# Two tile pairs without blocks at the start of two swiglu layers, and their block sums cut into steps

## The chip, the cores and the metric

One of the cores of one Trainium2 chip runs the kernel. The metric is the device time of one execution in microseconds (us), as the median of several runs. TensorE (PE) multiplies matrices, VectorE (DVE) and ScalarE (ACT) do the elementwise work, SyncE (SP) issues the loads of weights. "PEld" in the profile is TensorE loading the stationary operand.

## The reference

A block of a diffusion transformer with two layers works on 256 latent and 256 context tokens of width 1024, in float32. Each layer has a swiglu, a mixer (a short convolution in layer 0, grouped-query attention in layer 1) and another swiglu. Before each stands a modulated RMS norm, after each a gated residual sum.

```python
def _modulate(t, g, shift, scale):
    return _rms(t, g) * (1 + scale) + shift

def _swiglu(h, w13, w2):
    gte, up = jnp.split(h @ w13, 2, axis=-1)
    return (jax.nn.silu(gte) * up) @ w2
...
lat = lat + 0.5 * mod[:, 0, 2] * _swiglu(_modulate(lat, norm_g[i, 0], ...), ffn_w13[i, 0], ffn_w2[i, 0])
```

The hidden width is 2816, that is 22 tiles of 128 for the gate and 22 for the up part. The four swiglu layers are, in order of time, (layer 0, first), (layer 0, second), (layer 1, first), (layer 1, second). The first three work on all 512 tokens, the last on the 256 latent ones.

## The kernel before

The activations stand transposed: 128 features on the partitions, tokens along the free axis; the 512 tokens are two halves s = 0 (latent) and s = 1 (context). Every float32 product is made of three fast ones: each operand is split into a high part (ScalarE copies it to the rounded type) and a low part (VectorE subtracts the high part), `split` at L91 to L93, and `mm3` (L112 to L118) issues high*high, high*low and low*high. A product in the text below is one of these three matmuls.

A swiglu runs over the hidden tiles in thirds of 8, 7 and 7. "Tile pair" i is gate tile i and up tile i. `ffn` (L600) makes a pair in one of two ways.

- Without blocks: `load_w` loads and splits the weights (1024 x 256), `w13_mm` (L511) runs over the eight 128-deep slices of the 1024 features, for gate (`pg`) and up (`pu`): 2 x 8 x 3 = 48 products for each token half of 256 columns, 96 in all. `w13_post` (L517) takes silu, multiplies and splits the result.
- With blocks: `Pair` (L525) uses Winograd's form of Strassen's algorithm on 2 x 2 blocks: weights A11, A12, A21, A22 (feature half by gate or up), operand blocks B[feature half, token half]. It needs seven block products of 4 x 3 = 12 matmuls, 84 in all, and sums of blocks: S1 to S4 of the weights (VectorE, L548 to L557, into the tile `ws`, of which there is one), T1 to T4 of the operand (`Blocks.sums`, L314 to L330). Its steps are `head` (A11*B00 and A12*B10, first token half alone), `five` (S1*T1), `six` (S2*T2, S4*B11), `seven` (S3*T3) and `four` (A22*T4). `p` and `q` are its accumulators.

The operand blocks come from the norm before: `tail_norm` (L386) queues work that `flush` runs later. For s = 0 the blocks are made while the projection before still runs its last products; for s = 1 `both_parts` (L409) makes the inverse norm (TensorE sums squares, L231, ScalarE takes the root, VectorE the reciprocal, TensorE spreads it, L242), then two blocks (`block`, L290: VectorE scales to `t`, ScalarE adds the shift and writes `hr`, `bh` and VectorE `bl`), then all block sums.

The second and third swiglu (`ffn(0, 1, ...)` and `ffn(1, 0, ...)`) start at L607 with one pair without blocks: its first token half, then `flush` (the whole norm of s = 1 and the sums), then the next two pairs are loaded, split and summed and their heads run, then the second token half of the first pair. The first swiglu doesn't take this branch, nor does the last.

Buffers: three for raw weights (`wr`), four for halves of split weights (`wh`, `wl`), two for A22 (`w4h`, `w4l`), 16 for operand blocks and their sums, six PSUM banks for accumulators (one each for pg, pu, p, q). Loads are issued by SyncE in the program's order, each when its buffer is free. The text of the kernel gives the order of priority; a scheduler then sets each engine's fixed order, in which the engine works, and the semaphores. So the order of the lines is not that of the instructions. The modulation vectors are reduced on VectorE (L136) in spare places (`tick`).

Of the kernel before, what the change touches and what calls it, by code (L numbers as in the profile page):

```python
# [9 lines left out]
F32 = mybir.dt.float32  # L10
# [6 lines left out]
P = 128  # L17
D = 1024
KT = D // P
S = 256  # L20
# [19 lines left out]
def hybrid_kernel(ctx: ExitStack, tc: tile.TileContext, a: dict, out: bass.AP):  # L40
# [13 lines left out]
    def nm(s):  # L54
        uid[0] += 1
        return f"{s}{uid[0]}"
# [29 lines left out]
    def load_raw(src, n=2048):  # L86
        raw = wp.tile([P, 2048], F32, name=nm("wr"), tag="wr", bufs=3)
        nc.sync.dma_start(raw[:, :n], src)
        return raw
# [194 lines left out]
    class Blocks:  # L284
# [26 lines left out]
        def blk(self, key, k):  # L311
            return tuple(t[:, k * S : k * S + S] for t in self.t[key])

        def sums(self):  # L314
            r = self.raw
            b11, b12, b21, b22 = r[0, 0], r[0, 1], r[1, 0], r[1, 1]
            tt = nc.vector.tensor_tensor

            def keep(key, src):
                hi, lo = self.t[key] = hot("th"), hot("tl")  # L320
                split(hi, lo, src)

            tt(out=b11, in0=b12, in1=b11, op=ALU.subtract)
            keep("T1", b11)
            tt(out=b12, in0=b22, in1=b12, op=ALU.add)
            tt(out=b22, in0=b22, in1=b11, op=ALU.add)
            keep("T2", b22)
            tt(out=b21, in0=b21, in1=b22, op=ALU.subtract)
            keep("T3", b12)
            keep("T4", b21)  # L330

    class FirstBlocks(Blocks):

# [52 lines left out]
    def tail_norm(l, j, h):  # L386

        box = {}

        def tail(m, c0, c1):  # L390
            square_add(m, c0, c1)
            if m == KT - 1:
                if not box:
                    box["A"] = scale_of(l, j)
                    box["B"] = mod_ready(l, 3 * j)
                s = c0 // S

                def inv():
                    return rms_inv(s, (accs[s], accs[s, "last"]))

                def rest(part, ri):

                    if isinstance(h, Blocks):
                        h.block(s, part, box["A"], box["B"], ri, fine=s == 0 and part == 0)
                    else:
                        for k in range(4 * part, 4 * part + 4):
                            norm_k(s, k, h, box["A"], box["B"], ri)

                def both_parts():  # L409
# [115 lines left out]
    class Pair:  # L525
# [4 lines left out]


        def __init__(self, src, h):
            self.h = h
            raw = load_raw(src)
            a21, a22, a11, a12 = (raw[:, i * T2 : i * T2 + T2] for i in range(4))
            tt = nc.vector.tensor_tensor
            sm = wp.tile([P, 2048], F32, name=nm("ws"), tag="ws", bufs=1)
            s1, s2, s3, s4 = (sm[:, i * T2 : i * T2 + T2] for i in range(4))
            self.w = {}

            def keep(keys, src):
                hi, lo = half()
                split(hi, lo, src)
                for i, key in enumerate(keys):
                    self.w[key] = [t[:, i * T2 : i * T2 + T2] for t in (hi, lo)]

            keep(("A11", "A12"), raw[:, 1024:])
            tt(  # L548
                out=sm.rearrange("p (a b c) -> p a b c", a=2, b=2)[:, :, 0, :],
                in0=a21.unsqueeze(1).to_broadcast([P, 2, T2]),  # L550
                in1=raw[:, T2 : 3 * T2].rearrange("p (a c) -> p a c", a=2),
                op=ALU.subtract,
            )
            tt(out=s2, in0=a11, in1=s1, op=ALU.subtract)
            keep(("S1", "S2"), sm[:, :1024])
            tt(out=s4, in0=a12, in1=s2, op=ALU.subtract)
            keep(("S3", "S4"), sm[:, 1024:])  # L557
# [42 lines left out]
    def ffn(l, b, h, tot, gate, tail, gs=(), ev=1.5):  # L600
        gs = list(gs)
        i0 = 0
        for t, n in enumerate(THIRDS):
            between = ()
            if tot == T2:
                heads = []
                if t == 0 and not gs:  # L607

                    w = load_w(a["w13"][l, b, 0])
                    gs = [new_pair("g")]  # L610
                    pp = psum("pg"), psum("pu")
                    w13_mm(pp, w, h, range(KT), 0, S)
                    flush()
                    for i in (1, 2):
                        heads.append(Pair(a["w13"][l, b, i], h))
                        heads[-1].head()
                    w13_mm(pp, w, h, range(KT), S, T2)
                    w13_post(pp, gs[0], 0, T2)
                prev = None
                for i in range(len(gs), n):  # L620
                    if t == 0 and not heads and i in AS_IS[l, b]:
                        w = load_w(a["w13"][l, b, i])
                        pp = psum("pg"), psum("pu")
# [543 lines left out]
```

## Time and profile before

| | us |
|---|---|
| median of 3 runs | 1614.27 (1613.15 to 1616.92) |
| profiled execution | 1611.37 |
| its span, first to last instruction | 1609.5 |
| second swiglu: first product to fourth pair's first product | 569.82 to 607.11 |
| third swiglu: the same | 924.40 to 963.06 |

A page of the profile gives each engine's busy time and share, the chain of work that ended last (followed back from the last instruction) and the costliest groups of instructions. The views by time have one row for a run of equal instructions: start, time from the first's start to the last's end, engine, line, operation, output<-inputs, sizes, count, and in brackets the idle time before it and what ended that. The view by windows has, for each stretch, its length, then busy time and count of each engine, the clock that TensorE was granted (1.00 is full speed), the share of the DMA engines in use and GB/s. Matmul records overlap in time: one of 128x256 is shown with 0.28 us, while the next starts 0.12 us later.

### The profile page before, as it was taken

The numbers are of one execution on the slowest core, as the hardware profiler recorded it, in microseconds if no ns is written. First come the engines' busy times: TensorE is split into PE (matmuls) and PEld (weight loads), VectorE is DVE, ScalarE is ACT, GpSimd is POOL, SyncE is SP. The second block draws the span as 40 slices with busy tenths as digits, with TensorE's granted clock in tenths as the row PEclk, the third lists the DMA queues.
The fourth block names the chain that finished last, engine by engine and source line by source line (L and its number), as shares of the span: only waits on it lengthen the run. The fifth ranks groups of instructions, "written<-read, shape, count | busy, mean of one in ns | idle before, by whom it ended". The sixth has DMA issues, their size and how long they took to land.

```text
span 1609.5 us, 25613 instructions
## 1 busy us (share of the span) xinstructions
PE 1576.1 (98%) x10566; PEld 1450.1 (90%) x10566; DVE 1332.4 (83%) x2035; ACT 722.2 (45%) x1110; POOL 0.2 (0%) x4
## 2 busy tenths in 40 slices
PE   9999999999999999999999999999999999899999
PEld 6788998999888889899899889889899897789999
DVE  4988778879998889799797999898898789965554
ACT  5532452544322365335255465245254455454443
POOL 0000000000000000000000000000000000000000
PEclk9999999999999999999999999999999999999999
DMA  8456235234565513353433413452432463755453
GB/s 320 162 183 209 80 122 180 90 135 152 177 221 186 180 41 117 132 183 100 168 120 115 154 54 131 172 195 96 156 129 96 180 214 108 270 201 185 169 194 109
DMA packets 38277, 248.77 MB, mean 155 GB/s; under 512 B 5136, under 2 KB 6928, under 8 KB 12304
## 3 DMA queue, kind: packets, MB, share of 16 engines
q1 hardware_dynamic: 35712, 245.38, 43.7%
q10 hardware_dynamic: 2448, 1.76, 0.4%
q8 instruction: 82, 1.34, 0.3%
q14 instruction: 35, 0.29, 0.1%
HBM read 244.77 MB, written 1.05 MB: 153 GB/s over the span
## 4 chain that ended last, share of the span: by engine, by line
PE 82%; DVE 12%; DMA 3%; ACT 2%; issue 1%; DVEq 0%; ACTq 0%; SPq 0%
PE py L117 7%; PE py L116 7%; PE py L118 7%; PE p L116 6%; PE p L118 6%; PE p L117 6%; PE q L118 5%; PE q L116 5%; PE q L117 5%; DVE junk L136 4%; DVE wl L93 3%; PE pg L117 2%; PE pg L118 2%; PE pg L116 2%; PE pu L117 2%; PE pu L118 2%
## 5 line engine op out<-in xcount | busy, mean ns | idle before, releaser
L92 ACT ACTIVATE wh<-wr 128x1024 fp32r<-128x1024 f32 (+2 forms) x274 | 274.4, 1014 | 395.0 <-PE py L117 108.7
L93 DVE TENSOR_TENSOR wl<-wr,wh 128x1024 fp32r<-128x1024 f32 (+2 forms) x274 | 318.2, 1167 | 97.0 <-ACT wh L92 96.4
L136 DVE CUSTOM_DVE_ANT_0 junk<-wr,scbc,modb 128x1024 bf16<-128x1024 f32 x236 | 302.5, 1282 | 39.6 <-DMA wr<-in_modT 37.0
L117 PE MATMUL py<-gl,wh 128*128 128x512 f32 (+1 forms) x746 | 263.2, 353 | 0.0
L116 PE MATMUL py<-gh,wh 128*128 128x512 f32 (+1 forms) x746 | 263.1, 353 | 0.0
L118 PE MATMUL py<-gh,wl 128*128 128x512 f32 (+1 forms) x746 | 262.9, 352 | 0.0
L93 DVE TENSOR_TENSOR wl<-ws,wh 128x1024 fp32r<-128x1024 f32 x112 | 136.8, 1223 | 27.3 <-ACT wh L92 27.0
L118 PEld LDWEIGHTS py<-gh,wl 128*128 128x128 f32 x746 | 141.1, 189 | 19.1
L116 PEld LDWEIGHTS py<-gh,wh 128*128 128x128 f32 x746 | 141.2, 189 | 18.6
L117 PEld LDWEIGHTS py<-gl,wh 128*128 128x128 f32 x746 | 141.2, 189 | 18.0
L92 ACT ACTIVATE wh<-ws 128x1024 fp32r<-128x1024 f32 x112 | 117.8, 1057 | 76.4 <-PE p L117 34.2
L116 PE MATMUL p<-th,wh 128*128 128x256 f32 x448 | 126.8, 283 | 0.0
L117 PE MATMUL p<-tl,wh 128*128 128x256 f32 x448 | 126.8, 283 | 0.0
L118 PE MATMUL p<-th,wl 128*128 128x256 f32 x448 | 126.6, 283 | 0.0
L117 PE MATMUL q<-bl,wh 128*128 128x256 f32 x336 | 95.2, 283 | 0.0
L116 PE MATMUL q<-bh,wh 128*128 128x256 f32 x336 | 95.1, 283 | 0.0
L118 PE MATMUL q<-bh,wl 128*128 128x256 f32 x336 | 95.1, 283 | 0.0
L438 DVE SCALAR_TENSOR_TENSOR x<-py,G,x 128x256 f32<-128x256 f32 x168 | 74.2, 480 | 21.4 <-PE py L118 21.2
L116 PEld LDWEIGHTS p<-th,wh 128*128 128x128 f32 x448 | 86.0, 192 | 0.5 <-ACT sg L584 0.2
L117 PEld LDWEIGHTS p<-tl,wh 128*128 128x128 f32 x448 | 86.0, 192 | 0.3
L118 PEld LDWEIGHTS p<-th,wl 128*128 128x128 f32 x448 | 85.9, 192 | 0.0
L116 PE MATMUL pg<-hh,wh 128*128 128x256 f32 (+1 forms) x240 | 75.8, 316 | 4.6 <-ACT hh L260 4.6
(236 smaller groups left out, 4001.3 us busy)
## 6 DMA issues: line engine op xcount, KB each, us to landing
wr<-in_w SPq DMA_DIRECT2D x88, 1024.0 KB, 4.9
wr<-in_modT SPq DMA_DIRECT2D x67, 1024.0 KB, 4.9
wr<-in_w2b SPq DMA_DIRECT2D x32, 896.0 KB, 4.6
wr<-in_w2a SPq DMA_DIRECT2D x16, 1024.0 KB, 4.9
wr<-in_cw_cx SPq DMA_DIRECT2D x8, 1024.0 KB, 4.9
wr<-in_mod SPq DMA_DIRECT2D x5, 1024.0 KB, 7.4
wr<-in_cw_b SPq DMA_DIRECT2D x4, 1024.0 KB, 4.8
wr<-in_cw_out SPq DMA_DIRECT2D x4, 1024.0 KB, 4.9
```

The lines of the kernel that those rows point to most:

```text
L92: nc.scalar.activation(out=hi, in_=src, func=AF.Copy)
L93: nc.vector.tensor_tensor(out=lo, in0=src, in1=hi.bitcast(F32), op=ALU.subtract)
L116: nc.tensor.matmul(ps, wh, mh, start=first, stop=False, **kw)
L117: nc.tensor.matmul(ps, wh, ml, start=False, stop=False, **kw)
L118: nc.tensor.matmul(ps, wl, mh, start=False, stop=last, **kw)
L136: nc.vector.tensor_tensor_reduce(out=junk, in0=raw[:, j * D : j * D + D], in1=scbc[:, v, :], scale=1.0, scalar=modb[:, l, col : col + 1], ...
L438: nc.vector.scalar_tensor_tensor(out=x[:, m, s * S : s * S + S], in0=ps[:, o : o + S], scalar=g[:, m, s : s + 1], in1=x[:, m, s * S : s * ...
```

## The change

The second and third swiglu begin with two pairs without blocks (0 and 1) and one head (pair 2), instead of one and two. The order of priority is now: first half of pair 0, norm of s = 1, load of pair 1 and its first half, T1; second half of pair 0; load of pair 2, T2, S1 and S2; second half of pair 1; head of pair 2, T3 and T4, S3 and S4 and A22. Both kinds of sums are cut into steps that the caller names (`sums(n)`), and the norm no longer makes the operand's sums itself.

```diff
-        def sums(self):
+        def sums(self, n):
...
+            if n == 0:
+                tt(out=b11, in0=b12, in1=b11, op=ALU.subtract)
+                keep("T1", b11)
+            elif n == 1:
+                tt(out=b12, in0=b22, in1=b12, op=ALU.add)
+                tt(out=b22, in0=b22, in1=b11, op=ALU.add)
+                keep("T2", b22)
+            else:
+                tt(out=b21, in0=b21, in1=b22, op=ALU.subtract)
+                keep("T3", b12)
+                keep("T4", b21)
...
                     for part in range(2):
                         rest(part, ri)
-                    if isinstance(h, Blocks):
-                        h.sums()
...
         def __init__(self, src, h):
-            self.h = h
-            raw = load_raw(src)
...
+            self.h, self.w = h, {}
+            self.raw = load_raw(src)
+            self.keep(("A11", "A12"), self.raw[:, 1024:])
...
+        def sums(self, n):
...
+            if n == 0:
+                self.sm = sm = wp.tile([P, 2048], F32, name=nm("ws"), tag="ws", bufs=1)
...
+                self.keep(("S1", "S2"), sm[:, :1024])
+                return
+            sm = self.sm
+            tt(out=sm[:, 3 * T2 :], in0=a12, in1=sm[:, T2:1024], op=ALU.subtract)
+            self.keep(("S3", "S4"), sm[:, 1024:])
...
-                    w = load_w(a["w13"][l, b, 0])
-                    gs = [new_pair("g")]
-                    pp = psum("pg"), psum("pu")
-                    w13_mm(pp, w, h, range(KT), 0, S)
+                    w = [load_w(a["w13"][l, b, 0])]
+                    gs = [new_pair("g") for _ in range(2)]
+                    pp = [(psum("pg"), psum("pu")) for _ in range(2)]
+                    w13_mm(pp[0], w[0], h, range(KT), 0, S)
                     flush()
-                    for i in (1, 2):
-                        heads.append(Pair(a["w13"][l, b, i], h))
-                        heads[-1].head()
-                    w13_mm(pp, w, h, range(KT), S, T2)
-                    w13_post(pp, gs[0], 0, T2)
+                    w.append(load_w(a["w13"][l, b, 1]))
+                    w13_mm(pp[1], w[1], h, range(KT), 0, S)
+                    h.sums(0)
+                    w13_mm(pp[0], w[0], h, range(KT), S, T2)
+                    w13_post(pp[0], gs[0], 0, T2)
+                    heads.append(Pair(a["w13"][l, b, 2], h))
+                    h.sums(1)
+                    heads[0].sums(0)
+                    w13_mm(pp[1], w[1], h, range(KT), S, T2)
+                    w13_post(pp[1], gs[1], 0, T2)
+                    heads[0].head()
+                    h.sums(2)
+                    heads[0].sums(1)
...
                         pr = Pair(a["w13"][l, b, i0 + i], h)
+                        pr.sums(0)
+                        pr.sums(1)
                         pr.head()
```

More of the change, by code (lines that the diff above doesn't have):

```diff
@@ L321, in keep @@
                 split(hi, lo, src)
[L323 to L330, printed above, removed]
+            if n == 0:
[9 more added lines that the diff above has]
+                keep("T4", b21)
     class FirstBlocks(Blocks):
@@ L532, in __init__ @@
         def __init__(self, src, h):
-            self.h = h
-            raw = load_raw(src)
-            a21, a22, a11, a12 = (raw[:, i * T2 : i * T2 + T2] for i in range(4))
-            tt = nc.vector.tensor_tensor
[L537 to L557, printed above, removed]
+            self.h, self.w = h, {}
@@ new lines, in __init__, with keep @@
+            self.raw = load_raw(src)
+            self.keep(("A11", "A12"), self.raw[:, 1024:])
+        def keep(self, keys, part):
+            hi, lo = half()
+            split(hi, lo, part)
+            for i, key in enumerate(keys):
+                self.w[key] = [t[:, i * T2 : i * T2 + T2] for t in (hi, lo)]
+        def sums(self, n):
+            a21, a22, a11, a12 = (self.raw[:, i * T2 : i * T2 + T2] for i in range(4))
+            tt = nc.vector.tensor_tensor
+            if n == 0:
+                self.sm = sm = wp.tile([P, 2048], F32, name=nm("ws"), tag="ws", bufs=1)
+                tt(
+                    out=sm.rearrange("p (a b c) -> p a b c", a=2, b=2)[:, :, 0, :],
+                    in0=a21.unsqueeze(1).to_broadcast([P, 2, T2]),
+                    in1=self.raw[:, T2 : 3 * T2].rearrange("p (a c) -> p a c", a=2),
+                    op=ALU.subtract,
+                )
+                tt(out=sm[:, T2:1024], in0=a11, in1=sm[:, :T2], op=ALU.subtract)
+                self.keep(("S1", "S2"), sm[:, :1024])
[3 more added lines that the diff above has]
+            self.keep(("S3", "S4"), sm[:, 1024:])
```

## Prediction

> **What bounds the kernel now.** I read the page first: span, busy line, chain of work that ended last.
>
> ```profile
> span 1609.5 us, 25613 instructions
> PE 1576.1 (98%) x10566; PEld 1450.1 (90%) x10566; DVE 1332.4 (83%) x2035; ACT 722.2 (45%) x1110; POOL 0.2 (0%) x4
> PE 82%; DVE 12%; DMA 3%; ACT 2%; issue 1%; DVEq 0%; ACTq 0%; SPq 0%
> ```
>
> TensorE is nearly always busy and holds 82% of the chain, so a change gains only where TensorE stands or runs slowly. The view by windows shows the two stretches that the change rewrites, from the first product of a swiglu to the first product of its fourth tile pair. They differ from an ordinary stretch (608 to 618).
>
> ```profile
> core 0: us, PE busy (x) PEld busy (x) DVE busy (x) ACT busy (x) POOL busy (x), PEclk, DMA share, GB/s
> 569.80:607.10 37.30, 33.76 (x254) 32.61 (x253) 32.24 (x43) 25.18 (x41) 0.00 (x0) 0.91 0.17 57
> 583.20:589.00 5.80, 5.25 (x23) 4.96 (x24) 5.80 (x7) 3.72 (x7) 0.00 (x0) 0.50 0.00 0
> 608.00:618.00 10.00, 10.00 (x84) 9.95 (x84) 9.96 (x14) 6.11 (x10) 0.00 (x0) 1.00 0.31 107
> 924.40:963.10 38.70, 35.08 (x255) 33.54 (x254) 35.42 (x48) 25.89 (x44) 0.00 (x0) 0.91 0.17 55
> 930.50:933.70 3.20, 3.20 (x15) 3.20 (x16) 3.20 (x5) 0.68 (x1) 0.00 (x0) 0.50 0.98 325
> 944.00:947.40 3.40, 3.27 (x15) 3.27 (x16) 3.40 (x5) 0.00 (x0) 0.00 (x0) 0.50 0.02 5
> ```
>
> An ordinary product (128x256) costs 10.00/84 = 0.119, say 0.12 us. Up to the fourth pair the program has 240 products in each stretch: 96 of the pair without blocks, 84 of the second, 60 of the third. That is 28.8 us; the stretches take 37.3 and 38.7. Part of the rest are waits, part the clock: in three windows the granted clock is 0.50 and a product takes twice as long. The timeline of TensorE names the waits of the second swiglu, the view of its waits from 924 to 964 those of the third (total, times, longest).
>
> ```profile
> 579.95 0.28 PE L118 MATMUL q<-bh,wl 128*128 128x256 f32 x1
> 583.25 0.58 PE L116 MATMUL pg<-bh,wh 128*128 128x256 f32 x1 [3.03 <-ACT bh L92]
> 584.55 0.58 PE L117 MATMUL pg<-bl,wh 128*128 128x256 f32 x1 [0.49 <-DVE bl L93]
> ```
>
> ```profile
> PE ss L231 <- ACT sq L214: 1.2, 1, 1.2
> PE pg L117 <- DVE bl L93: 1.0, 2, 0.5
> PE pg L116 <- ACT bh L92: 0.6, 1, 0.6
> PE q L116 <- ACT th L92: 0.4, 1, 0.4
> PE ss L242 <- DVE ri L240: 0.3, 1, 0.3
> ```
>
> In the second swiglu TensorE runs out of products that need only the first token half and stands 3.03 us until the second half's block is split. In the third it stands 3.5 us in smaller pieces.
>
> **Products.** A tile pair without blocks is 96 products, one with blocks 84. One pair per swiglu changes kind: 12 more products, 1.44 us, twice: **+2.9 us**, certain. In exchange TensorE has more to do before it needs the second token half: 96 products of two pairs, where it had 48 of one pair and 24 of the next pair's head. 24 more are 2.9 us, about the length of the 3.03 us wait.
>
> **Second swiglu.** In the compiled order TensorE takes after its 24 products with the first block: four column sums, two products with the second block, two of the new pair, then the rest. TensorE takes products in order, so the two of the new pair hold all behind them. Now six products of the second pair's head (p) fill that place. The rows, of TensorE, ScalarE and VectorE:
>
> ```profile
> 572.58 0.28 PE L118 MATMUL pu<-bh,wl 128*128 128x256 f32 x1
> 572.70 0.28 PE L231 MATMUL ss<-ones,acc 128*128 128x1 f32 x2
> ...
> 578.30 0.60 PE L242 MATMUL ss<-ident,ri 128*128 128x128 f32 x4
> ```
>
> ```profile
> 572.88 0.40 ACT L214 ACTIVATE sq<-x 128x256 f32<-128x256 f32 x1
> 573.19 1.04 ACT L92 ACTIVATE bh<-hr 128x1024 fp32r<-128x1024 f32 x1
> 574.21 0.26 ACT L236 ACTIVATE rs<-ss,eps_t 128x2 f32<-128x2 f32 x1
> 574.37 1.05 ACT L92 ACTIVATE wh<-ws 128x1024 fp32r<-128x1024 f32 x1
> ```
>
> ```profile
> 574.27 1.23 DVE L93 TENSOR_TENSOR bl<-hr,bh 128x1024 fp32r<-128x1024 f32 x1 [0.67 <-ACT bh L92]
> 575.41 0.16 DVE L240 RECIPROCAL ri<-rs 128x2 f32<-128x2 f32 x1
> 575.49 1.20 DVE L93 TENSOR_TENSOR wl<-ws,wh 128x1024 fp32r<-128x1024 f32 x1
> ```
>
> The split of the new pair's second weight half takes the place of the one at 574.37. A weight split of the fourth pair (A22) now stands ahead of the first block on ScalarE and VectorE; its load is issued when the first pair's weights are split, as now, so it shifts that chain by no more than about 0.3 us. Hence the weights are ready at 574.37 + 1.05 + 0.3 = 575.7. From 572.7 TensorE has four column sums (0.28 each by the row, 1.1) and two products (0.24) to do in 3.0 us: **1.65 us of new idle time**. After that nothing is late: the weights' low part is ready near 577.0 (575.49 + 1.20 + 0.3) and needed near 579.2 (22 products and the transposes, 0.6, after 575.9); TensorE then has 46 products, to 584.7, while the second half's block, ready at 583.20 and 584.5 now (rows above), comes 0.3 to 0.9 earlier, because two splits of sums of weights (1.2 us each on VectorE) no longer stand between its steps. The waits of 3.03 and 0.49 go. With them goes the slow clock of 583 to 589: 23 products, 2.8 us at 0.12, kept TensorE 5.25 us, so 2.5 us. Sum: 1.44 + 1.65 - 3.5 - 2.5 = **-2.9 us**, if no new slow window comes.
>
> ```profile
> 926.90:930.30 3.40, 2.04 (x16) 1.64 (x14) 2.65 (x6) 2.88 (x8) 0.00 (x0) 1.00 0.01 2
> 940.55:943.96 3.41, 2.05 (x13) 1.44 (x11) 3.41 (x4) 2.52 (x3) 0.00 (x0) 1.00 0.00 0
> ```
>
> These are the 3.4 us just before the slow windows at 930.5 and 944: 2.04 and 2.05 us busy was enough for the clock to fall. In the changed kernel the 3.4 us around the new idle time are about as busy, so I give a slow window there an even chance. One costs 3.4 us at 15 products (1.8 us): 1.6 us. The bounds are -2.9 and -1.3; I take the middle, **-2.1**. [...]
>
> **Third swiglu.** The waits of 3.5 us go, since the first-half products of two pairs are enough until the second half's blocks are split, and with them both slow windows: 30 products, 3.6 us, took 6.5: 2.9 us. 1.44 us come on top. New waits: ScalarE's second weight split stands right behind the first quarter of the first block and waits for its buffer, held by the projection's last product at about 924.5. Everything behind it on ScalarE (three quarters of that block, the next block) stands with it, and VectorE, which needs their results, too.
>
> ```profile
> 922.04 0.68 DVE L556 TENSOR_TENSOR ws<-wr,ws 128x512 f32<-128x512 f32 x1
> 922.64 1.26 DVE L250 SCALAR_TENSOR_TENSOR t<-x,A,ss 128x256 f32<-128x256 f32 x3
> ```
>
> ```profile
> 923.31 0.90 ACT L299 ACTIVATE bh<-t,mod 128x256 fp32r<-128x256 f32 x2
> ```
>
> The split (1.05) ends near 925.6, and ScalarE's steps of 0.4 us run on from there instead of 923.7. TensorE follows in order: 0.1 for that split, 0.35 for the second quarter's high part (926.4), 0.25 for its low part, 0.45 for the new pair's first low weights (VectorE, behind that quarter's low part: 928.1), 0.45 for the second (behind the norm's reciprocal: near 932.3); small ones make it 1.8 us. VectorE's subtraction for the third pair (the 0.68 row's place is taken by one of 1.22) delays the first t by 0.3, within that. Sum: 1.44 + 1.8 - 3.5 - 2.9 = **-3.2**. Followed from start to end instead (924.4, 252 products of 0.12, 1.7 for sums and transposes, 1.8 waits) the stretch ends at 958.1 against 963.1: -5.0. The two differ by small gaps of the present run that I can't name and that may remain. Bounds -3.2 and -5.0; I take **-4.1**.
>
> **At nothing:** VectorE and ScalarE lose the new pair's share (some 5 us on VectorE per swiglu: subtractions of weights, one and a half splits, three steps of its end); off the chain here, hidden beside 33 us of products. Two modulation reductions (1.28 each, below) move from the third swiglu's pairs to just before its norm; the norm's sums on TensorE end after them.
>
> ```profile
> L136 DVE CUSTOM_DVE_ANT_0 junk<-wr,scbc,modb 128x1024 bf16<-128x1024 f32 x236 | 302.5, 1282 | 39.6 <-DMA wr<-in_modT 37.0
> ```
>
> The block sums in their steps: the compiled order puts the first of them where it was, after the blocks; the first use comes later by 24 products or more, so they have over 3 us of slack. Outside the two stretches all orders are as before.
>
> **Sum:** -2.1 - 4.1 = -6.2 us. On the profiled execution, 1611.37 (1.9 around its span of 1609.5), that is 1605.2. The median shown is 1614.27, 2.9 higher, so I forecast **1608.1**.
>
> **Rivals.**
> - *The clock stays up, small gaps go too:* -2.9 - 5.0 = -7.9, **1606.4**. For it: each new wait but the first is shorter than those now. Against: the rows at 926.9 and 940.55. [...]
> - *Other waits take the place of the old:* the third swiglu's third load. SyncE's list of loads is the same in number and order; this one goes into the first pair's buffer and is issued at 916.54. VectorE's subtraction of it now stands ahead of the first block.
>
> ```profile
> 909.29 0.33 SPq L88 DMA_DIRECT2D wr<-in_w  x1
> ...
> 916.54 0.33 SPq L88 DMA_DIRECT2D wr<-in_w  x1
> ```
>
> ```profile
> 916.50 0.63 ACT L92 ACTIVATE w4h<-wr 128x512 fp32r<-128x512 f32 x1 [0.91 <-DMA wr<-in_w]
> ```
>
> ```profile
> wr<-in_w SPq DMA_DIRECT2D x88, 1024.0 KB, 4.9
> ```
>
>   At 4.9 it lands at 921.4, before its turn; at the 7.2 of the load of 909.29 at 923.7, 2 us late, with one slow window 3.6 us: -2.6 in all, **1611.7**. Behind it stand the block's steps, for which TensorE waits.
> - *No gain:* the sums stay where they were and the 2.9 us of products eat what is filled: **1614**.
> - *Slower: stalls moved, not filled.* The new pair's weights go through the same two queues as the blocks. If they are ready after the second half's block (583.2; I reckon 577.0, in the third near 932 against 940), the waits of 3.5 + 3.5 stay, 2.9 is paid, and each stretch has one slow window more: 2.9 + 3.2 = +6.1, **1620.4**. For it: VectorE is busy 35.42 of 38.7 us. Against: these splits stand ahead of that block's on both engines.
>
> **How the numbers follow.** A measurement tells 0.2% (3.2 us) from no change. Forecast (-4 to -8) 0.50; clock stays up 0.17; other waits 0.18, of which 0.07 beyond 3.2 us; no gain 0.06; slower 0.09. Faster 0.50 + 0.17 + 0.07 = 0.74, same 0.11 + 0.06 = 0.17, slower 0.09. The range leaves a tenth on each side: 1603.5 (the clock's rival and 2.9 more, the scatter between the profiled execution and the median) to 1614 (no gain).
>
> **What would show it.** The wait for bh at the second swiglu (3.03) is gone; instead some 1.7 us before a pg product, for wh on ScalarE. The stretches to the fourth pair last 35.2 and 34.6 us. At most one window at 0.50 in the first, none in the second. 24 more products. It is wrong if TensorE still waits over 1 us for the second half's blocks, if the third swiglu's first block starts over 1 us later, or if a half-clock window follows in both.

## The result, and the profile after

The changed kernel takes 1606.18 us, the median of four executions (1604.79 to 1607.14); the kernel before, in four on the same chip, 1613.71 (1612.65 to 1616.92). The ratio is 0.9946, with a 95% interval of 0.9928 to 0.9963. By the medians that is 7.5 us less, by the ratio 8.7 (6.0 to 11.6); the forecast was 6.2 less. The time is 1.9 below the forecast and inside its range, 0.6 of that because the kernel before came out at 1613.71 and not at 1614.27. On another chip, beside the last experiments, it was 1605.73 against 1614.83, a ratio of 0.9937 (0.9922 to 0.9952). The ratios are not quite the quotients of the medians; gains below that are given with a range are worked out from the ratios.

The page of the profiled execution (1606.83 us) of the changed kernel: span, busy line, chain of work that ended last.

```profile
span 1605.0 us, 25629 instructions
PE 1578.0 (98%) x10590; PEld 1451.0 (90%) x10590; DVE 1322.5 (82%) x2021; ACT 717.7 (45%) x1100; POOL 0.2 (0%) x4
PE 88%; DVE 8%; ACT 1%; DMA 1%; issue 1%; ACTq 0%; SPq 0%; DVEq 0%
```

TensorE has the 24 products more (10590 for 10566), VectorE 14 instructions and 9.9 us less. TensorE's share of the chain goes from 82 to 88%. That is some 90 us, far more than was gained: the chain runs through other instructions than before, and its shares don't measure the gain.

The view by windows of the two rewritten stretches, first product to the fourth pair's first product:

```profile
core 0: us, PE busy (x) PEld busy (x) DVE busy (x) ACT busy (x) POOL busy (x), PEclk, DMA share, GB/s
572.28:607.21 34.93, 33.61 (x266) 33.23 (x265) 28.41 (x38) 23.30 (x38) 0.00 (x0) 0.95 0.18 61
923.54:957.36 33.82, 33.07 (x266) 31.94 (x265) 32.51 (x47) 25.60 (x42) 0.00 (x0) 1.00 0.20 68
```

37.29 became 34.93 us, 38.66 became 33.82: -2.4 and -4.8, together -7.2. Each holds 11 or 12 product records more than before and is still shorter; the granted clock rose from 0.91 to 0.95 and 1.00. TensorE's waits, first in the second swiglu's stretch, then in the third's:

```profile
PE pg L116 <- ACT wh L92: 0.7, 1, 0.7
PE ss L231 <- ACT sq L214: 0.5, 1, 0.5
```

```profile
PE pg L118 <- DVE wl L93: 0.4, 1, 0.4
PE pu L118 <- DVE wl L93: 0.2, 1, 0.2
```

The waits for the second half's norm and blocks (3.03 + 0.49, and 3.5 in pieces) are gone; 1.2 and 0.6 us of others stand in their place.

The two profiled executions differ by only 4.5 us, less than the stretches' 7.2. Of the 2.7 us between, 2.5 are clock near the start, which the change leaves alone; the parts between and behind the two stretches differ by -1.0 and +1.2. The same 6.8 us near the start, in the kernel before and in the changed one:

```profile
14.83:21.66 6.83, 6.75 (x33) 2.92 (x34) 1.98 (x5) 1.50 (x4) 0.00 (x0) 1.00 0.85 289
```

```profile
14.83:21.66 6.83, 5.91 (x14) 1.79 (x15) 2.06 (x4) 1.54 (x4) 0.00 (x0) 0.50 0.83 295
```

14 matmuls against 33 in the same time: from 30 us on the changed kernel's TensorE is 2.5 us behind, up to its second swiglu (572.28 against 569.82). So what the change does has to be read from the stretches, and from medians.

### The profile page after: what moved, and what is told of

It reads as the page before. It is cut to its first block, busy times and chain, and to the rows that moved or that the text cites. A ratio compares the mean times of both kernels' runs of the same rounds, so it can differ in the third digit from the quotient of the medians.

```text
span 1605.0 us, 25629 instructions
## 1 busy us (share of the span) xinstructions
PE 1578.0 (98%) x10590; PEld 1451.0 (90%) x10590; DVE 1322.5 (82%) x2021; ACT 717.7 (45%) x1100; POOL 0.2 (0%) x4
## 3 DMA queue, kind: packets, MB, share of 16 engines
q1 hardware_dynamic: 35712, 245.38, 43.6%
## 4 chain that ended last, share of the span: by engine, by line
PE 88%; DVE 8%; ACT 1%; DMA 1%; issue 1%; ACTq 0%; SPq 0%; DVEq 0%
PE py L117 9%; PE py L116 9%; PE py L118 9%; PE p L118 6%; PE p L117 6%; PE p L116 6%; PE q L118 5%; PE q L116 5%; PE q L117 5%; DVE junk L136 3%; PE pg L116 2%; PE pg L117 2%; PE pg L118 2%; PE pu L118 2%; PE pu L117 2%; PE pu L116 2%
## 5 line engine op out<-in xcount | busy, mean ns | idle before, releaser
L136 DVE CUSTOM_DVE_ANT_0 junk<-wr,scbc,modb 128x1024 bf16<-128x1024 f32 x236 | 301.8, 1279 | 33.7 <-DMA wr<-in_modT 31.0
L93 DVE TENSOR_TENSOR wl<-ws,wh 128x1024 fp32r<-128x1024 f32 x108 | 131.7, 1223 | 29.0 <-ACT wh L92 28.9
L92 ACT ACTIVATE wh<-ws 128x1024 fp32r<-128x1024 f32 x108 | 113.5, 1058 | 68.7 <-PE p L117 35.5
L118 PE MATMUL p<-th,wl 128*128 128x256 f32 x432 | 122.3, 283 | 0.0
L117 PE MATMUL p<-tl,wh 128*128 128x256 f32 x432 | 122.2, 283 | 0.0
L116 PE MATMUL p<-th,wh 128*128 128x256 f32 x432 | 122.2, 283 | 0.0
L116 PE MATMUL q<-bh,wh 128*128 128x256 f32 x320 | 90.6, 283 | 0.0
L117 PE MATMUL q<-bl,wh 128*128 128x256 f32 x320 | 90.6, 283 | 0.0
L118 PE MATMUL q<-bh,wl 128*128 128x256 f32 x320 | 90.6, 283 | 0.0
```

The lines of the kernel that those rows point to most:

```text
L92: nc.scalar.activation(out=hi, in_=src, func=AF.Copy)
L93: nc.vector.tensor_tensor(out=lo, in0=src, in1=hi.bitcast(F32), op=ALU.subtract)
L116: nc.tensor.matmul(ps, wh, mh, start=first, stop=False, **kw)
L117: nc.tensor.matmul(ps, wh, ml, start=False, stop=False, **kw)
L118: nc.tensor.matmul(ps, wl, mh, start=False, stop=last, **kw)
L136: nc.vector.tensor_tensor_reduce(out=junk, in0=raw[:, j * D : j * D + D], in1=scbc[:, v, :], scale=1.0, scalar=modb[:, l, col : col + 1], ...
```

## Experiments

Below, a stretch runs to the **fifth** pair's first product, since some kernels put the fourth pair's head early. Windows are the stretches of 3.4 us in it at a granted clock of 0.50 (the changed kernel's one lasts from 578.03 to 581.44). Times are medians; each ratio is against the kernel before on the same chip and at the same time, whose median was 1614.11 us beside the four from second_only to pairs_alone, 1615.02 beside more_vector and the three that begin with norm_first, and 1614.83 beside mixed, after_again and three_plain. The stretches are those of one profiled execution each (pairs_alone's was the slowest of its six, more_vector's the fastest of its eight).

| kernel | ratio (95%) | median us | second: us (windows) | third: us (windows) |
|---|---|---|---|---|
| before | | 1613.71 | 47.51 (2) | 48.74 (2) |
| changed | 0.9946 (0.9928 to 0.9963) | 1606.18 | 45.20 (1) | 43.91 (0) |
| second_only | 0.9982 (0.9972 to 0.9993) | 1610.91 | 45.06 (1) | 48.75 (2) |
| third_only | 0.9970 (0.9956 to 0.9984) | 1609.08 | 47.71 (2) | 43.90 (0) |
| steps_alone | 1.0001 (0.9992 to 1.0009) | 1614.12 | 47.89 (1) | 48.21 (1) |
| pairs_alone | 0.9952 (0.9935 to 0.9969) | 1605.85 | 45.41 (1) | 44.14 (0) |
| more_vector | 0.9975 (0.9963 to 0.9986) | 1610.71 | 45.88 (0) | 46.26 (0) |
| norm_first_old | 0.9964 (0.9951 to 0.9978) | 1609.63 | 45.20 (0) | 46.57 (0) |
| norm_first_steps | 0.9971 (0.9959 to 0.9984) | 1611.13 | 43.26 (0) | 48.13 (1) |
| norm_first | 0.9936 (0.9924 to 0.9949) | 1605.40 | 44.90 (1) | 43.93 (0) |
| mixed | 0.9950 (0.9933 to 0.9967) | 1607.26 | 43.24 (0) | 43.92 (0) |
| after_again | 0.9937 (0.9922 to 0.9952) | 1605.73 | 45.22 (1) | 43.93 (0) |
| three_plain | 0.9963 (0.9948 to 0.9978) | 1608.77 | 44.87 (0) | 46.25 (1) |
| before_again | one run | 1613.93 | 47.07 (1) | 48.89 (2) |

One half-clock window costs some 1.6 us where TensorE has work throughout it (the changed kernel's holds 15 products in 3.4 us, 1.8 at 0.12), less where it also waits in it (before's two, 582.15 to 588.98, cost 2.6 together: TensorE is busy 5.23 us there at 0.50).

**The two halves of the change.** `second_only` has the new start under `l == 0`, `third_only` under `l == 1`, and the other start as before.

```diff
+                    if l == 0:    # third_only: l == 1
+                        w = [load_w(a["w13"][l, b, 0])]
...
+                    else:
+                        w = load_w(a["w13"][l, b, 0])
...
```

> Only the second swiglu has the new start, the third keeps the old one. Theory (filling): two pairs without blocks give TensorE 96 products of the first token half before it needs the second half's block, at a price of 12 products (1.44 us); the gain sits in the stretch itself. Then the second swiglu's stretch falls from 37.3 to about 34.9 us, with one wait of about 0.7 us for wh before a pg product and no wait for bh of 3 us, the third swiglu's stays at 38.7, and the time falls by 2.4 us against the kernel before (1 to 3.5). Rival (clock luck): the gain is that of half-clock windows that happen to fall elsewhere; then the stretch without its half-clock products (some 34.8 us in both) would not differ, and the whole could as well be 0 or -5. Rival (relief): the gain is the work that VectorE no longer does in both swiglus, about equal shares, -3.7 each.

> Only the third swiglu has the new start, the second keeps the old one. Theory (filling): the third swiglu's stretch falls from 38.7 to about 33.8 us, the second's stays near 37.3 with its wait of about 3 us for bh, and the time falls by 4.8 us against the kernel before (3.2 to 5.5); with the other half alone the two sum to the whole's -7.2 to -7.5. Rival (clock luck): the sum of the two halves misses the whole by 2 us or more. Rival (relief): -3.7, as in the other half.

Measured: -2.9 us (1.1 to 4.5) and -4.8 (2.6 to 7.1), from the ratios; the sum is -7.7, the whole by its ratio -8.7 (6.0 to 11.6). The windows of second_only, then of third_only:

```profile
573.78:618.84 45.06, 43.75 (x351) 43.24 (x349) 38.00 (x49) 28.89 (x47) 0.00 (x0) 0.96 0.21 71
924.90:973.65 48.75, 45.14 (x338) 43.59 (x337) 45.31 (x61) 31.46 (x53) 0.00 (x0) 0.93 0.19 66
```

```profile
573.13:620.84 47.71, 44.17 (x339) 42.97 (x337) 42.39 (x56) 31.32 (x50) 0.00 (x0) 0.93 0.20 67
927.71:971.61 43.90, 43.17 (x350) 42.04 (x349) 41.83 (x58) 31.30 (x51) 0.00 (x0) 1.00 0.23 78
```

Each half does what it does in the whole, and only there: the gain is local and adds up. Equal shares of 3.7 us would still fit both ranges of the times, but not the stretches, which fall by 2.5 and 4.8; with that goes the simplest form of the rival that VectorE's smaller load makes the gain. How much of the third's 4.8 is clock is told under norm_first_old.

**The pairs, or the steps.** `pairs_alone` keeps two pairs without blocks but makes the sums at once (and puts the block pair's head ahead of the second halves); `steps_alone` keeps one pair and two heads but makes the sums in steps, T1, S1 and S2 ahead of the second head and the rest behind both heads.

```diff
 # pairs_alone
                     flush()
+                    for n_ in range(3):
+                        h.sums(n_)
                     w.append(load_w(a["w13"][l, b, 1]))
...
 # steps_alone
                     w13_mm(pp, w, h, range(KT), 0, S)
                     flush()
+                    heads.append(Pair(a["w13"][l, b, 1], h))
+                    heads[0].head()
+                    h.sums(0)
+                    heads[0].sums(0)
+                    heads.append(Pair(a["w13"][l, b, 2], h))
+                    heads[1].head()
                     w13_mm(pp, w, h, range(KT), S, T2)
...
```

> Two pairs without blocks and one head as in the changed kernel, but the operand's sums stand all together right behind the norm in the order of priority, and the weights' sums behind their load, as before. Theory (filling): the steps do nothing of themselves, because the sums are needed only after 192 products; stretches within 1 us of the changed kernel's 34.9 and 33.8, time -7 us against the kernel before (-5.5 to -8.5). Rival (steps): the sums made at once hold up VectorE's split of the new pair's weights and of the blocks; TensorE waits 2 us or more in each start and the gain is 0 to -3.

> Both swiglus begin, as before, with one pair without blocks and two heads, but the sums are made in steps and the two heads stand ahead of the sums in the order of priority. No product is added, VectorE has all the work of the kernel before. First-half products ahead of the second half's block: 48 + 24 + 24 = 96, as with two plain pairs. Theory (filling): the wait of 3 us in the second swiglu goes, and 2 to 3 us of those of the third; what follows is that five of the first block pair asks for T1 and S1 only 48 products (5.7 us) after the second half's block, while VectorE has those sums still to make, so part comes back as waits there: -3 to -8 us in all, that is near the changed kernel without its price of 2.9. Rival (relief): without VectorE's work taken away (10 us less in the changed kernel) the waits only move to the sums: 0 to -1.5 us, stretches of 36.5 to 38.7 us with VectorE busy 32 to 35 of them. Rival (two plain pairs needed because the weights of the third head come too late): TensorE waits 1.5 us or more before p or q of that head.

The pairs alone bring it all, -7.7 us (5.0 to 10.5); the steps alone nothing (+0.2, -1.3 to +1.5). The steps are not needed where two pairs stand in front. But steps_alone also has 96 products of the first half ahead of the second half's block, and that theory's -3 to -8 failed. Its four largest waits on TensorE in the second stretch, and the rows of TensorE and VectorE that explain them:

```profile
PE p L117 <- DVE tl L93: 1.3, 1, 1.3
PE p L116 <- ACT wh L92: 1.1, 1, 1.1
PE pg L117 <- DVE bl L93: 0.7, 1, 0.7
PE p L118 <- DVE wl L93: 0.5, 1, 0.5
```

```profile
580.58 0.60 PE L242 MATMUL ss<-ident,ri 128*128 128x128 f32 x4
```

```profile
577.68 0.16 DVE L240 RECIPROCAL ri<-rs 128x2 f32<-128x2 f32 x1
577.76 1.20 DVE L93 TENSOR_TENSOR wl<-ws,wh 128x1024 fp32r<-128x1024 f32 x1
581.23 2.05 DVE L250 SCALAR_TENSOR_TENSOR t<-x,A,ss 128x256 f32<-128x256 f32 x5 [2.27 <-PE ss L242]
```

The waits moved to the third head's weights (wh, wl) and to the sums (tl). And the reciprocal of the norm is ready at 577.84, but the two products that spread it (L242) stand behind 22 others in TensorE's order and start at 580.58; VectorE stands 2.27 us, and all its later work, for which TensorE then waits, is late by that. The kernel before has 2.3 us of this idle time as well, and the prediction doesn't speak of it.

**VectorE's load put back.** `more_vector` is the changed kernel with some 5.4 us of idle work for VectorE in each start, an estimate from 0.68 us for a 128x512 subtraction at L557; by the windows VectorE is busy 4.0 us longer in the second stretch than in the changed kernel (41.98 against 38.02) and 3.3 in the third (45.16 against 41.83).

```diff
                     h.sums(1)
+                    for i_ in range(8):
+                        nc.vector.tensor_tensor(
+                            out=spare, in0=h.raw[0, 0][:, :512], in1=h.raw[1, 0][:, 512:], op=ALU.add
+                        )
                     heads[0].sums(0)
```

> The changed kernel with eight additions of 512 columns (0.68 us each, about 5.4 us) put on VectorE in each of the two starts, behind T2 in the order of priority; their result isn't used. So TensorE has the products of two pairs, and VectorE the load of the kernel before again. Theory (products alone): TensorE has enough first-half products, the load costs nothing: 1606 us, stretches 34.9 and 33.8. Theory (products and room on VectorE together, as the sums in steps with one pair gave no gain): in the second swiglu VectorE is busy 28.4 of 34.9 us and takes most of it, 0 to +2; in the third it is busy 32.5 of 33.8 us and gives back +3 to +5; in all 1609 to 1612. Rival (relief alone): all of the gain is given back in both, 1613 to 1616.

1610.71 us: some 4 us of the gain remain (ratio 0.9975 against 0.9937 and 0.9946 for the change itself), between "nothing" and "all". The windows and, from the second swiglu, TensorE's waits:

```profile
571.32:617.20 45.88, 42.74 (x351) 41.96 (x349) 41.98 (x56) 28.72 (x46) 0.00 (x0) 1.00 0.20 70
923.26:969.52 46.26, 43.68 (x351) 42.15 (x349) 45.16 (x65) 31.40 (x51) 0.00 (x0) 1.00 0.21 73
```

```profile
PE q L118 <- DVE wl L93: 1.1, 1, 1.1
PE q L116 <- ACT wh L92: 0.8, 1, 0.8
PE pg L116 <- ACT wh L92: 0.7, 1, 0.7
PE ss L231 <- ACT sq L214: 0.5, 1, 0.5
```

Both stretches have the full clock, so the added load costs 46.26 - 43.91 = 2.4 us in the third and, with the 1.6 of the changed kernel's window taken off, 45.88 - (45.20 - 1.6) = 2.3 in the second. The last two waits are the changed kernel's own; the first two are new and stand behind the start, at the fourth pair, whose weights VectorE and ScalarE now split too late. I had expected the second swiglu to take most of the load (0 to 2 us) and the third to give back 3 to 5; both pay alike. So the products fill the early waits, and the room that they leave on VectorE keeps the later ones away. This is one load at one place in VectorE's order; what it would cost elsewhere isn't shown.

**The norm earlier.** In three kernels `flush()` (the norm of the second half) stands ahead of the first half's products: with the start of before, with that of steps_alone, and with the changed one.

```diff
+                    flush()
                     w13_mm(pp[0], w[0], h, range(KT), 0, S)
-                    flush()
```

> The start of before (one pair without blocks, two heads, sums at once), with one line moved: the norm of the second token half is queued ahead of the first half's products, so that in the second swiglu TensorE's two products that spread the inverse norm stand 22 products earlier. No product is added, VectorE's work is that of before. Theory (TensorE stands because the second half's block is late): in the second swiglu the block comes about 2.5 us earlier, the wait of 3.0 us for bh falls below 1 us and with it one or two half-clock windows: -2 to -5 us, all in the second swiglu; the third's order in its first 100 products is that of before, so 0 there. Rival (VectorE is the bound): the waits move to the sums, time as before.

> One pair without blocks, two heads, sums in steps (the kernel that gave no gain), with the norm of the second half queued ahead of the first half's products as well. No product is added. Theory: in the second swiglu VectorE stood 2.3 us and more for the spread norm on TensorE; now it goes on, the third head's weights and T1 and T2 come 2 to 3 us earlier and the waits of 1.1, 0.7 and 1.3 us for them shrink: the second stretch to the fifth pair falls from 47.9 to 44.5 us, below the changed kernel's 45.2, since it has no price of 1.44; the third stays at 48.2. In all -3 to -4 us against the kernel before. Rival (VectorE's amount of work is the bound): 0 to -1.

> The changed kernel with the norm of the second half queued ahead of the first half's products. Theory (filling): in the changed kernel TensorE no longer waits for the second half's blocks, so blocks that come earlier bring nothing of themselves: within 1 us of the changed kernel in both stretches, but for the half-clock window of the second start (1.6 us), which the shorter wait ahead of it may or may not bring; 1604.5 to 1607. Rival (VectorE's place in time is the bound): the second stretch gains 2 to 3 us more, 1603.

Measured: -5.8 us (3.6 to 7.9), -4.7 (2.6 to 6.6) and -10.3 (8.2 to 12.3). In norm_first_steps the second stretch falls from 47.89 to 43.26 us, as that theory had it and by more (1.6 of it is the half-clock window that goes). VectorE's rows, TensorE's two products and TensorE's waits there:

```profile
578.66 1.21 DVE L93 TENSOR_TENSOR wl<-ws,wh 128x1024 fp32r<-128x1024 f32 x1
579.78 2.44 DVE L250 SCALAR_TENSOR_TENSOR t<-x,A,ss 128x256 f32<-128x256 f32 x6
```

```profile
578.96 0.60 PE L242 MATMUL ss<-ident,ri 128*128 128x128 f32 x4
```

```profile
PE p L116 <- ACT wh L92: 0.8, 1, 0.8
PE q L118 <- DVE wl L93: 0.7, 1, 0.7
PE p L117 <- DVE tl L93: 0.3, 1, 0.3
```

VectorE goes on without a gap. Net of its one half-clock window the changed kernel's second stretch is 45.20 - 1.6 = 43.6; so here the same is reached, and a little more, **without the 12 products more**. In the third swiglu the line changes nothing (48.13 against 48.21), and two pairs without blocks remain better by 4.2 us, 2.6 net of a window. norm_first, on the changed start, is within 0.3 us of the changed kernel in both stretches, as expected: TensorE no longer waits for the second half's blocks there.

norm_first_old was expected to lose its waits for the second block. It didn't: by the view of waits TensorE still stands 2.9 us in the second stretch (for bl 1.6, tl 0.8, sg 0.5). What went is the half clock: 45.20 us at 1.00 against 47.51 at 0.93. Its third stretch is the most instructive of all. The orders of the engines there are those of the kernel before, but for one column sum, and so are TensorE's waits (the prediction shows them for before; here norm_first_old's):

```profile
PE ss L231 <- ACT sq L214: 1.2, 1, 1.2
PE pg L117 <- DVE bl L93: 1.0, 2, 0.6
PE pg L116 <- ACT bh L92: 0.6, 1, 0.6
PE q L116 <- ACT th L92: 0.4, 1, 0.4
PE ss L242 <- DVE ri L240: 0.3, 1, 0.3
```

The view by windows of that stretch, in before:

```profile
924.40:973.14 48.74, 45.12 (x339) 43.58 (x337) 45.33 (x61) 31.46 (x53) 0.00 (x0) 0.93 0.20 66
```

The same in norm_first_old, with 3.4 us around each of two idle places:

```profile
923.79:970.36 46.57, 42.85 (x338) 40.84 (x337) 45.13 (x61) 31.60 (x53) 0.00 (x0) 1.00 0.21 69
925.06:928.48 3.42, 2.23 (x19) 2.03 (x18) 3.34 (x8) 3.42 (x9) 0.00 (x0) 1.00 0.02 5
938.72:942.13 3.41, 2.23 (x15) 1.62 (x13) 3.41 (x4) 2.51 (x3) 0.00 (x0) 1.00 0.00 0
```

48.74 against 46.57 us for the same work and the same waits: 2.2 us are the clock. In before its changes lie on a grid: it falls to 0.50 at 582.15, 930.31 and 943.96 us and is back at 1.00 at 588.98, 933.73 and 947.37, each a whole number of steps of 3.413 us from the one before (2, 100, 1, 3 and 1; 348.16 us from the first fall to the second are 102 steps). In the changed kernel it rises at 21.66 and falls at 578.03, 163 such steps apart. In before the two idle places fell into windows of the grid with 2.04 and 2.05 us of TensorE busy, and the clock fell; in norm_first_old, whose clock is 1.00 through the whole stretch, so that the grid isn't seen in it, TensorE was busy 2.23 us in each of the two rows above, and it stayed. That the grid's place made the difference is the author's estimate; it fits these two and isn't shown by them; more follows below.

**The kernels before and after once more, a mixture, and three pairs.** `mixed` takes norm_first_steps' start for the second swiglu and norm_first's for the third; `three_plain` makes pair 2 without blocks as well and begins blocks with pair 3.

```diff
 # three_plain
-                    gs = [new_pair("g") for _ in range(2)]
+                    gs = [new_pair("g") for _ in range(3)]
...
+                    heads.append(Pair(a["w13"][l, b, 3], h))
+                    w13_mm(pp[2], w[2], h, range(KT), 0, S)
                     heads[0].sums(0)
+                    w13_mm(pp[2], w[2], h, range(KT), S, T2)
+                    w13_post(pp[2], gs[2], 0, T2)
```

> Three pairs without blocks at the start of both swiglus, then one head. Theory (price): 12 products more per swiglu at 0.12 us, 1.44 us each, and nothing left to fill, so +2.9 us against the changed kernel, 1607.5 to 1610, the larger end if no half-clock window goes; 48 products of a pair more and VectorE idle more. Rival (the more of VectorE's work goes, the better): 1603 to 1605, below the changed kernel.

> The changed kernel once more, beside the others on the same chip: -7.5 us against the kernel before (-5.5 to -9.5). For the clock: its half-clock window at the second start was on a grid of 3.41 us; if the grid lies otherwise against the work in this execution, so that no window of the grid holds more than 0.8 us of TensorE's idle time there, it is absent and the second stretch is 33.3 us to the fourth pair instead of 34.9.

> The kernel before once more, for its clock: the two half-clock windows in the third swiglu's start cost 2.2 us to the fifth pair (48.7 with them, 46.6 in a kernel whose first 100 products there have the same order, without them). Theory (grid): whether they come depends on where a free grid of 3.41 us falls; with 1.36 us or more of idle time in one window of the grid the clock fell there, with 1.18 it didn't. So 48.7 or 46.6 us, by the idle time in the windows of this execution's grid. Rival (the waits alone decide): 48.7 us again, whatever the grid.

> The second swiglu starts with one pair without blocks, two heads, sums in steps and the norm of the second half queued first (43.25 us to the fifth pair in its own run); the third starts with two pairs without blocks and the norm first (43.93). If the two starts are independent, as the two halves of the change were, the second stretch is 43.2 to 43.5 us to the fifth pair, the third 43.9 to 44.2, and the time 9.5 to 11 us below the kernel before, 1.5 to 2 below the changed kernel. Rival (the saving of 12 products is eaten by the waits for the third head's weights, 0.8 and 0.7 us): no more than the changed kernel, -7.5.

three_plain: a median of 1608.77, 3.0 us above after_again's on the same chip (4.2 by the ratios), as the price of 2 x 1.44 has it; more relief for VectorE brings nothing once the waits are filled. Net of a window of 1.6 the stretches are 1.3 and 0.7 us longer than the changed kernel's.

after_again repeats both stretches within 0.02 us, window included (granted clock 0.96 and 1.00 in both), so it doesn't tell what another place of the grid would do; the 0.8 us in its expectation is the author's estimate, which no run tested. Of the six profiles of a second start with two pairs without blocks five have one window (0.96 over the stretch); more_vector's, with the same waits of 0.7 and 0.5 us, has none (1.00). In the 3.41 us before the clock fell TensorE was busy 2.15 us in the changed kernel and 2.58 in norm_first; how more_vector's waits lie against the grid isn't shown.

before_again had its two windows in the third start again (48.89 us), behind grid windows with 1.87 and 1.93 us busy, as the grid's theory has it (2.04 and 2.05 in before; 2.23 in norm_first_old, where it stayed); but its grid lay nearly as in before (the first fall 6.13 us behind the start, there 5.91), so the rival that the waits alone decide would say the same of this one run, and in the third start only norm_first_old speaks against it. And idle time in a grid window isn't the whole rule. The first two rows are of before: behind one the clock fell, behind the other, as empty as those of the third start, it stayed at 1.00 (1066.84 to 1070.26). The third is of before_again, the same place of the same start as the first (from 8.9 us behind its first product), and here the clock stayed at 1.00 in the next window (the stretch's only one at 0.50 is 588.15 to 591.57). The last two are of norm_first (it fell):

```profile
578.74:582.15 3.41, 1.49 (x13) 1.28 (x11) 2.85 (x6) 2.65 (x6) 0.00 (x0) 1.00 0.00 0
1063.43:1066.84 3.41, 2.05 (x15) 1.84 (x15) 3.41 (x5) 2.42 (x4) 0.00 (x0) 1.00 0.80 250
```

```profile
581.33:584.74 3.41, 1.53 (x13) 1.33 (x12) 2.80 (x6) 2.64 (x5) 0.00 (x0) 1.00 0.00 0
```

```profile
573.20:576.61 3.41, 2.58 (x19) 2.08 (x17) 2.73 (x4) 3.41 (x8) 0.00 (x0) 1.00 0.00 0
576.61:580.02 3.41, 3.03 (x14) 3.03 (x15) 2.95 (x7) 1.16 (x4) 0.00 (x0) 0.50 0.32 43
```

What decides it stays open.

mixed has the two stretches that were expected, 43.24 and 43.92 us, 2 us less than the changed kernel in the second. Its time isn't the expected one: 1607.26, six executions from 1603.87 to 1609.99, in two groups of three; the lower three, 9.7 to 11.0 us below the kernel before, lie where all were expected. In the profiled one, of the upper group, 312.54 us lie between the stretches, 306.06 in norm_first. ScalarE's wait for a load near 910 in mixed, what TensorE made of it, and the same load's wait in norm_first:

```profile
ACT wh L92 <- DMA wr<-in_w: 4.6, 1, 4.6
...
PE ss L231 <- DVE acc L222: 3.2, 1, 3.2
```

```profile
ACT wh L92 <- DMA wr<-in_w: 2.1, 1, 2.1
```

The weights of the mixer's projection came 2.5 us later (the loads were issued alike, from 905.15 us on and from 905.64 in norm_first, but took a median of 7.2 us to land against 4.9), the norm before the third swiglu with them, TensorE stood 3.2 us and two half-clock windows followed (0.50 from 918.64 to 925.46). Whether the second start's new timing brings that on, or chance, three executions of each kind don't tell. The fastest kernel by its median is norm_first, 1605.40, which can't be told from the changed one.

## Why the prediction was right

- **Products, +2.9:** right: 24 more in the profile, and three_plain's further 24 cost 3.0 us by the medians.
- **Second swiglu, -2.1** (-2.9 to -1.3): -2.4. The waits of 3.03 and 0.49 went, the wait for wh on ScalarE came, and the "even chance" of a half-clock window fell out the dear way in five profiles of six. With the window the sum gives -1.3, not -2.1, so the measured time is 1.1 better than the sum and lies near the middle by luck. The 1.1 lies at the waits. Reckoned from the start of one product to the start of the next, the kernel before lost 4.8 us at waits and around them (47.51 less 324 products of 0.12, 1.2 for column sums and transposes and 2.6 of slow clock), the changed one 1.9 (45.20 less 336 products, 1.5 and 1.6): 3.0 less, where the sum has 3.5 - 1.65 = 1.85 less. The new idle time was 1.2 us, not 1.65: the split ended 5.8 us after the start, as reckoned (5.9), but TensorE got to it later, since its column sums had themselves stood 0.53 us for a square:

```profile
575.96 0.38 PE L231 MATMUL ss<-ones,sq 128*128 128x1 f32 x2 [0.53 <-ACT sq L214]
...
577.13 0.28 PE L116 MATMUL pu<-bh,wh 128*128 128x256 f32 x1
578.09 0.58 PE L116 MATMUL pg<-bh,wh 128*128 128x256 f32 x1 [0.68 <-ACT wh L92]
```

The grid window with both waits in it, behind which the clock fell to 0.50:

```profile
574.62:578.03 3.41, 2.15 (x16) 1.77 (x15) 2.74 (x4) 3.41 (x7) 0.00 (x0) 1.00 0.02 5
```

- **The clock in the second start:** it has no wait of TensorE over 0.68 us, and the clock fell to 0.50 at 578.03 all the same. The measurement decides: the term of -2.9, which holds if no new slow window comes, didn't come.
- **Third swiglu, -4.1** (-3.2 to -5.0): -4.8, near the bound that was followed from start to end (33.7 us for the stretch, 33.8 measured). By the view of waits the new ones are 0.6 us, not 1.8: 0.2 for the new pair's first low weights and 0.4 for the second, of 0.45 reckoned for each. But that view counts only the idle time between records, and a record of 0.28 us outlasts the 0.12 to the next start. From start to start, the delays of 0.35 and 0.25 for the second quarter came too, smaller: the products that need its high and its low part start 0.34 and 0.30 us behind the one before them, not 0.12:

```profile
925.53 0.38 PE L116 MATMUL pg<-bh,wh 128*128 128x256 f32 x1
...
926.05 0.39 PE L117 MATMUL pg<-bl,wh 128*128 128x256 f32 x1
```

To the fifth pair the changed kernel's 43.91 us hold 336 products of 0.12 (40.3) and column sums and transposes (1.3), so 2.3 are lost at waits and around them, where 1.8 was reckoned. norm_first_old's 46.57, the old waits at the full clock, hold 324 products (38.9) and the same 1.3, so 6.4 are lost there, where the bound of -3.2 took 3.5. That was the mis-sized term; the small gaps that the prediction couldn't name lie beside the waits. The slow clock's 2.9 is too large as well: norm_first_old shows 2.2 for two windows, and that they needn't come at all. Without them the gain in the third is 46.57 - 43.91 = 2.7 us.
- **At nothing:** VectorE's lost share was put down as hidden. more_vector shows that it isn't: given back, behind T2, it costs 2.3 to 2.4 us in each stretch, in waits behind the start. The relief is part of the gain, and the prediction had put it at nothing. That the steps are free was right (pairs_alone).
- **Rivals:** "stalls moved, not filled" is what steps_alone does: the waits go over to weights and sums, with no gain. In the changed kernel it didn't come, because the new pair's weights were ready in time, for the reason given. The third load wasn't late. "The clock stays up" has nearly the measured time (1606.4, nearer than the forecast), but not for its reason: the window in the second came, and the time beside the old waits, which its -2.9 left out as well, made up for it.

## What to carry to other kernels

Work that fills a wait must be ready, not only present: count what the other engines have to make for it, and look at what stands in their queues and in TensorE's. A wait of TensorE can begin with a pair of tiny products that sit behind 22 others in its own order (in steps_alone they start at 580.58, 2.74 us behind the reciprocal that they need); moving them up gave, in one stretch, as much as a second pair without blocks, and without its 12 products (47.89 us to 43.26, 3.0 net of the half-clock window). A view of waits counts idle time alone; price a wait by the starts of the products around it (here 6.4 us against 3.5 in the view). Compare stretches, with their half-clock windows counted, before believing a difference of under 3 us between two profiled executions.

## What was not expected of the hardware

In before the granted clock changes on a grid of 3.413 us: in the two starts its falls at 582.15, 930.31 and 943.96 us and its rises at 588.98, 933.73 and 947.37 are all whole multiples of it apart. The grid's place against the work isn't quite the same each time: the first fall in the third start came 5.91 us behind the first product in before, 6.13 in before_again. One order of instructions (but for one column sum) with the same waits ran 48.74 us with two half-clock windows (before) and 46.57 with none (norm_first_old). Idle time in a window doesn't decide alone: behind one with 1.53 us of TensorE busy the clock stayed up (before_again), behind one with 2.58 it fell (norm_first). And a start that held TensorE idle for only 1.2 us, in waits of 0.53 and 0.68, lost another 1.6 us to the half-clock window behind it (15 products in the 3.41 us from 578.03).
